# Experts 0 and 1: one x array with four tokens to a partition, loaded in two strided halves

## The chip, the cores and the metric

The kernel runs on one core of a Trainium2 chip. The metric is the device time of one execution in microseconds (us); lower is better. Every time below comes from runs on the chip or from one profiled execution of the kernel before.

## The reference

Eight experts, each a two-layer network with its own weights. Inputs are float32: x (8 x 256 x 512), w1 (8 x 512 x 2048), w2 (8 x 2048 x 512), b1 (8 x 2048), b2 (8 x 512).

```python
h = np.matmul(x, w1) + b1[:, np.newaxis, :]
h = np.maximum(h, 0)
return (np.matmul(h, w2) + b2[:, np.newaxis, :]).astype(np.float32)
```

The weights are 67 MB, 4.2 MB to each matrix; an x of one expert is 0.5 MB.

## The kernel before

**Weights.** GpSimd's queue loads every w1 and w2 by one DMA (the last two w2 by two), and the DMA casts float32 to float16 on the way. Three buffers each for w1 and w2 rotate (NW = 3), so a load of expert e >= 3 waits on GpSimd until TensorE is through with expert e - 3 (`load_w1`, `load_w2`, lines 147 to 162). The issue order of this queue is written out by hand in lines 164 to 175: w1 of 0, b2, w1 of 1, x of 2 and 3, w1 of 2, w1 of 3, w2 of 0, x of 4 to 7, w1 of 4, w2 of 1 and so on. The first of them waits for `s_first`, which ScalarE raises after its warm-up activation (line 126).

**x.** The x of experts 2 and 3 (one DMA) and of 4 to 7 (one DMA) also goes through GpSimd's queue, cast on the way. The x of experts 0 and 1 does not: SyncE loads it as float32 at the very start, one DMA of 512 KB for each expert (lines 129 to 131), two tokens to a partition, so that partition p of `x32[e]` holds tokens 2p and 2p + 1 in 4 KB. VectorE casts expert 0 (line 132) and ScalarE expert 1 (line 134).

**Turning x.** TensorE needs x with the hidden dimension on the partitions. `transposes(e)` (lines 108 to 123) does this on VectorE with 32 x 32 block transposes. `x16[e]` gives the array, its first partition and R, the tokens to a partition; one instruction turns R blocks by 4, so an expert takes T // R // 32 * 4 instructions: 16 for R = 2 (experts 0 and 1), 8 for R = 4 (experts 2 and 3), 4 for R = 8. Tokens come out in an order that depends on R, and `h_columns` (line 205) puts them in the order of the output when ScalarE evicts h.

**Order.** `transposes(0)` stands ahead of a section that is synchronised by hand (line 137), which every engine but GpSimd enters when the casts and turns ahead of it are done. In the section VectorE turns b1 (line 180), then x of expert 1, and in step s the x of expert s + 1 (line 201). Steps run from 0 to 10: step s does the first product of expert s (line 294, s < 8) and the second product of expert s - 3 (line 311, s >= 3); line 321 adds b2. SyncE stands between the DMAs and TensorE: in step s it waits for b2 (step 0), for the turned x (`s_xT`) and for w1 to land (line 235 in `go`), and then raises `s_go` for TensorE, which takes it in line 279. ScalarE evicts the first product with bias and ReLU (line 223) from four PSUM banks; its first eviction also waits for the turned b1. VectorE and ScalarE evict the second product (line 195). The results of experts 6 and 7 go into `x32[0]` and `x32[1]`, which are free by then (line 79), and are stored by SyncE (line 246); the results of 0 to 3 and of 4 and 5 are stored by two DMAs when the last weights are in (line 240).

Of the kernel before, what the change touches and what calls it, by code (L numbers as in the profile page):

```python
# [10 lines left out]
def kernel(  # L11
# [12 lines left out]
    nc = tc.nc  # L24
    fp32 = mybir.dt.float32
    fp16 = mybir.dt.float16
    relu = mybir.ActivationFunctionType.Relu
    PE = mybir.EngineType.PE
    E, T, H = x.shape
    M = w1.shape[2]  # L30
    P = 128
    nTB = T // P
# [15 lines left out]
    def sbuf(name, shape, dtype):  # L48
        return ctx.enter_context(nc.sbuf_tensor(name, shape, dtype))
# [11 lines left out]
    w2_sb = sbuf("w2_sb", [P, NW * nJ * H], fp16)  # L61
    xT = sbuf("xT", [P, 2 * nKC * T], fp16)
    hT = sbuf("hT", [P, (LAG + 1) * nJ * T], fp16)
    x32 = [sbuf(f"x32_{e}", [P, nTB, H], fp32) for e in range(2)]
    x16 = {}
    for e in range(2):
        x16[e] = (sbuf(f"x_{e}", [P, nTB, H], fp16), 0, nTB)
    x_group = {}
    for first, n in X_LOADS.items():
        R = n * T // P  # L70
# [3 lines left out]
    results = {}  # L74
    for first, n in GROUPS.items():
        t = sbuf(f"out_{first}", [P, n * nTB, H], fp32)
        for i in range(n):
            results[first + i] = t
    results[E - 2], results[E - 1] = x32
    ph = ctx.enter_context(nc.psum_tensor("ph", [P, NPH, H], fp32))  # L80
    po = ctx.enter_context(nc.psum_tensor("po", [P, 2 * nTB * H], fp32))

# [25 lines left out]
    def transposes(e):  # L108
        t, p0, R = x16[e]
        if e >= 2:  # L110
            first = max(f for f in X_LOADS if f <= e)
            nc.vector.wait_ge(landed[f"x{first}"], 16)
            nc.vector.wait_ge(s_ph, nJ * (e - 1))
        mine = xT[:, e % 2 * nKC * T : (e % 2 + 1) * nKC * T].rearrange("p (kc t) -> p kc t", kc=nKC)
        last = None
        for g in range(T // R // B):
            src = t[p0 + B * g : p0 + B * (g + 1)]
            for b in range(nB):
                last = nc.vector.transpose(  # L119
                    out=mine[b * B : (b + 1) * B].rearrange("p kc (r g i) -> p g r kc i", r=R, i=B)[:, g],  # L120
                    in_=src[:, :, b * (H // nB) : (b + 1) * (H // nB)].rearrange(
                        "p r (i kc) -> p r kc i", kc=nKC))
        return last
# [2 lines left out]
    tc.keep_in_program_order(nc.scalar.activation(out=warm[:], in_=ones1[:], func=relu).then_inc(s_first, 1))  # L126
    tc.keep_in_program_order(nc.scalar.dma_start(
        out=b1_rows[:], in_=b1.rearrange("e (b i) -> (e b) i", b=nB)))
    for e in range(2):
        tc.keep_in_program_order(nc.sync.dma_start(  # L130
            out=x32[e][:], in_=x[e].rearrange("(p tb) h -> p tb h", tb=nTB)))
    nc.vector.tensor_copy(out=x16[0][0][:], in_=x32[0][:])  # L132
    transposes(0)
    tc.keep_in_program_order(nc.scalar.copy(out=x16[1][0][:], in_=x32[1][:]))  # L134

    section = ctx.enter_context(ExitStack())
    by_hand = section.enter_context(tc.tile_critical(
# [17 lines left out]
    def load_w2(e):  # L155
# [5 lines left out]
        for lo, hi in zip(cuts, cuts[1:]):  # L161
# [5 lines left out]
         in_=b2.rearrange("e h -> (e h)").rearrange("(o f) -> o f", o=1))  # L167
# [11 lines left out]
    for b in range(nB):  # L179
        turned = nc.vector.transpose(  # L180
            out=b1T[b * B : (b + 1) * B, nB - 1 - b : nB - 1 - b + nJ * B],
            in_=b1_rows[:].rearrange("r (i j) -> r j i", j=nJ),
# [31 lines left out]
    for s in range(E + LAG):  # L214
        if s < E:
            if s > LAG:
                nc.scalar.wait_ge(s_po, nTB * (s - LAG))
            for j in range(nJ):
# [5 lines left out]
                    out=dst,  # L224
                    in_=src,
# [22 lines left out]
    for s in range(E + LAG):  # L248
# [5 lines left out]
        e = s - LAG  # L254
# [114 lines left out]
```

## Time and profile before

| | |
|---|---|
| time, median of 3 runs | 180.75 us (180.69 to 181.15) |
| the profiled execution, its own time | 180.72 us |
| its span in the trace | 178.9 us |
| TensorE busy | 135.3 us, 76% |
| VectorE busy | 65.1 us, 36% |
| ScalarE busy | 75.4 us, 42% |
| DMA moved | 40.46 MB, mean 226 GB/s |

The span runs from the first to the last instruction that the profile holds; 1.8 us of the run lie outside it. In the profile, PE is TensorE's matmul, PEld its weight load, DVE is VectorE, ACT ScalarE, POOL GpSimd and SP SyncE; a "q" behind a name is that engine's sequencer. A group shows its line, engine, operation, output <- input and count; then its busy time, the mean duration in ns of one, and the idle time of the engine ahead of it with what ended that. GB/s counts the bytes as written, so a casting load reads twice what it shows.

### The profile page before, as it was taken

Reading aid. Unit: us, or ns where it says so; the run is one execution under the profiler, and the core shown is the slowest. Engines: PE = TensorE matmul, PEld = TensorE weight load, DVE = VectorE, ACT = ScalarE, POOL = GpSimd, SP = SyncE. Lnnn points to the kernel's source line nnn. Section 1 sums busy time; section 2 is a strip of 40 time slices with the busy share of each in tenths; the row PEclk is TensorE's granted clock in tenths of the full one; section 3 lists DMA queues with packets and bytes.
Section 4 is the critical chain, followed back from the end, with each engine's and each line's share of the span. In section 5 each row is a group of like instructions: output and inputs, shape, how many; then the busy total and the mean of one; then the engine's idle time right before and its main releaser. Section 6 shows DMA issues by size and latency. Waiting matters only on the chain. (4 is left out here: it accounts for less than half of the span.)

```text
span 178.9 us, 2979 instructions
## 1 busy us (share of the span) xinstructions
PE 135.3 (76%) x784; PEld 93.5 (52%) x784; DVE 65.1 (36%) x92; ACT 75.4 (42%) x153; POOL 11.7 (7%) x25
## 2 busy tenths in 40 slices
PE   0003988868699890998978896889698896999990
PEld 0003878858698330794468643874298442434330
DVE  0989938475000299700088006910230003030100
ACT  3201596757777113483087505780387201020110
POOL 4200012020200101001010001000200002000000
PEclk9999999999999997599999999999999999799999
DMA  5989989999999998998999999999899899999996
GB/s 201 282 179 233 234 178 233 234 194 218 236 209 200 236 220 190 234 231 179 234 231 194 220 234 212 198 234 220 190 234 231 183 231 205 212 227 201 348 416 266
DMA packets 3826, 40.46 MB, mean 226 GB/s; under 512 B 448, under 2 KB 464, under 8 KB 1264
## 3 DMA queue, kind: packets, MB, share of 16 engines
q0 software_dynamic: 2912, 35.14, 92.5%
q1 hardware_dynamic: 864, 5.24, 7.2%
q10 hardware_dynamic: 48, 0.07, 0.1%
q14 instruction: 2, 0.02, 0.0%
HBM read 71.39 MB, written 4.19 MB: 422 GB/s over the span
## 5 line engine op out<-in xcount | busy, mean ns | idle before, releaser
L294 PE MATMUL ph<-xT,w_sb 128*128 x512 | 72.4, 303 | 33.1 <-PEq L279 30.2
L294 PEld LDWEIGHTS ph<-xT,w_sb 128*128 x512 | 66.8, 146 | 39.8 <-issue 29.1
L223 ACT ACTIVATE hT<-ph,b1T 128x256 f16<-128x256 f32 x128 | 60.1, 474 | 33.4 <-PE ph L294 29.8
L311 PE MATMUL po<-w_sb,hT 128*128 x256 | 58.3, 387 | 1.8 <-issue 1.8
L119 DVE STREAM_TRANSPOSE xT<-x 32x256 f16<-32x256 f16 (+2 forms) x64 | 45.0, 703 | 27.0 <-DMA x<-in_x_dram 22.4
L311 PEld LDWEIGHTS po<-w_sb,hT 128*128 x256 | 25.3, 99 | 34.1 <-issue 8.4
L195 DVE COPY out<-po 32x512 f32<-32x512 f32 (+1 forms) x20 | 13.7, 687 | 64.8 <-PE po L311 64.6
L195 ACT COPY out<-po 32x512 f32<-32x512 f32 (+1 forms) x20 | 11.5, 577 | 47.7 <-PE po L311 47.5
L88 POOL DMA_DIRECT2D w_sb<-in_w_dram x18 | 9.7, 541 | 137.2 <-PE po L311 71.4
L321 PE MATMUL po<-b_sb,ones 1*128 x16 | 4.8, 378 | 3.9 <-issue 2.5
L195 ACT COPY x<-po 128x512 f32<-128x512 f32 x2 | 1.2, 585 | 13.6 <-PE po L311 13.6
L195 DVE COPY x<-po 128x512 f32<-128x512 f32 x2 | 1.4, 692 | 13.3 <-PE po L311 13.3
L321 PEld LDWEIGHTS po<-b_sb,ones 1*128 1x128 f16 x16 | 1.3, 91 | 6.4 <-issue 6.1
L180 DVE STREAM_TRANSPOSE b1T<-b_rows 32x512 f32<-32x512 f32 x4 | 4.1, 1026 | 0.5 <-issue 0.5
L134 ACT CAST x<-x 128x1024 f16<-128x1024 f32 x1 | 1.0, 1044 | 3.4 <-DMA x<-in_x_dram 3.4
L132 DVE CAST x<-x 128x1024 f16<-128x1024 f32 x1 | 0.7, 695 | 3.2 <-DMA x<-in_x_dram 3.2
L126 ACT ACT_TABLE_LOAD x1 | 1.3, 1283 | 0.7 <-PEq L353 0.7
L88 POOL DMA_DIRECT2D x<-in_x_dram x2 | 1.3, 664 | 0.0
L88 POOL DMA_DIRECT2D b_sb<-in_b_dram x1 | 0.5, 499 | 0.0
L125 DVE MEMSET ones<- 1x128 f16 x1 | 0.2, 165 | 0.9 <-PEq L353 0.9
L126 ACT ACTIVATE warm<-ones 1x128 f16<-1x128 f16 x1 | 0.3, 309 | 0.0
L353 POOL MEMSET const-float32-0.0<- 128x1 f32 x1 | 0.1, 99 | 0.2 <-issue 0.2
(3 smaller groups left out, 0.3 us busy)
## 6 DMA issues: line engine op xcount, KB each, us to landing
w_sb<-in_w_dram POOLq DMA_DIRECT2D x14, 2048.0 KB, 41.1
w_sb<-in_w_dram POOLq DMA_DIRECT2D x2, 1024.0 KB, 27.1
out_dram<-out SPq DMA_DIRECT2D x1, 2048.0 KB, 7.2
w_sb<-in_w_dram POOLq DMA_DIRECT2D x1, 1536.0 KB, 17.7
x<-in_x_dram SPq DMA_DIRECT2D x2, 512.0 KB, 4.1
x<-in_x_dram POOLq DMA_DIRECT2D x1, 1024.0 KB, 34.3
out_dram<-out SPq DMA_DIRECT2D x1, 1024.0 KB, 9.3
out_dram<-x SPq DMA_DIRECT2D x2, 512.0 KB, 6.4
```

The source lines that it names most:

```text
L88: engine.dma_start(**kw).then_inc(landed[key], 16)
L119: last = nc.vector.transpose(out=mine[b * B : (b + 1) * B].rearrange("p kc (r g i) -> p g r kc i", r=R, i=B)[:, g], in_=src[:, :, b * (H / ...
L125: nc.vector.memset(ones1[:], 1.0)
L126: tc.keep_in_program_order(nc.scalar.activation(out=warm[:], in_=ones1[:], func=relu).then_inc(s_first, 1))
L132: nc.vector.tensor_copy(out=x16[0][0][:], in_=x32[0][:])
L134: tc.keep_in_program_order(nc.scalar.copy(out=x16[1][0][:], in_=x32[1][:]))
L180: turned = nc.vector.transpose(out=b1T[b * B : (b + 1) * B, nB - 1 - b : nB - 1 - b + nJ * B], in_=b1_rows[:].rearrange("r (i j) -> r j i" ...
L195: last = copy(out=results[e][at : at + rows, tb * n + k, :], in_=po[k * rows : (k + 1) * rows, bank : bank + H])
L223: nc.scalar.activation(out=dst, in_=src, func=relu, bias=b1T[:, bias_at : bias_at + 1], scale=1.0,).then_inc(s_credit, 1)
L294: last = nc.tensor.matmul(ph[:, j % NPH, 0:T], w1_sb[:, bass.ds(w_from + (kc * M + j), P, nJ)], xT[:, bass.ds(x_at + kc * T, T)], start=(k ...
L311: return nc.tensor.matmul(banks[tb], hT[:, bass.ds(h_from + (j * nTB + tb) * P, P)], w2_sb[:, bass.ds(w2_from + j * H, H)], start=False, s ...
L321: nc.tensor.matmul(banks[tb], ones1[:], b2_sb[:, bass.ds(s * H, H)], start=True, stop=False)
```

## The change

Both x arrays become one: `x32` and `x_0` have 128 partitions of four tokens. Partitions 0 to 63 hold expert 0 and partitions 64 to 127 expert 1; partition p holds tokens 4p to 4p + 3 of its expert. SyncE still issues two DMAs of 512 KB. The first takes rows 0 and 1 of each partition, the second rows 2 and 3, so each reads 128 runs of 4 KB that lie 8 KB apart, and each brings half of both experts. VectorE casts the first half and ScalarE the second, and `transposes(0)`, which now reads partitions 0 to 63 in all four rows, stands behind both casts. R becomes 4 for experts 0 and 1, so `transposes` issues 8 instructions of the 32 x 512 form for each instead of 16 of the 32 x 256 form. The results of experts 6 and 7 go into the two halves of `x32`.

```diff
-    x32 = [sbuf(f"x32_{e}", [P, nTB, H], fp32) for e in range(2)]
-    x16 = {}
-    for e in range(2):
-        x16[e] = (sbuf(f"x_{e}", [P, nTB, H], fp16), 0, nTB)
+    R0 = 2 * nTB
+    x32 = sbuf("x32", [P, R0, H], fp32)
+    x16_0 = sbuf("x_0", [P, R0, H], fp16)
+    x16 = {e: (x16_0, e * (P // 2), R0) for e in range(2)}
+    x_halves = [(r, r + nTB) for r in range(0, R0, nTB)]
...
-    results[E - 2], results[E - 1] = x32
+    for e, (lo, hi) in zip((E - 2, E - 1), x_halves):
+        results[e] = x32[:, lo:hi, :]
...
-    for e in range(2):
-        tc.keep_in_program_order(nc.sync.dma_start(
-            out=x32[e][:], in_=x[e].rearrange("(p tb) h -> p tb h", tb=nTB)))
-    nc.vector.tensor_copy(out=x16[0][0][:], in_=x32[0][:])
+    x_rows = x[0:2].rearrange("e (p r) h -> (e p) r h", r=R0)
+    for lo, hi in x_halves:
+        tc.keep_in_program_order(nc.sync.dma_start(out=x32[:, lo:hi, :], in_=x_rows[:, lo:hi, :]))
+    (lo, mid), (_, hi) = x_halves
+    nc.vector.tensor_copy(out=x16_0[:, lo:mid, :], in_=x32[:, lo:mid, :])
+    tc.keep_in_program_order(nc.scalar.copy(out=x16_0[:, mid:hi, :], in_=x32[:, mid:hi, :]))
     transposes(0)
-    tc.keep_in_program_order(nc.scalar.copy(out=x16[1][0][:], in_=x32[1][:]))
```

## The prediction

> **What bounds the kernel now.** I read the page's DMA part first, then the chain that ended last, and then the timeline of the places that the chain names.
>
> ```profile
> DMA  5989989999999998998999999999899899999996
> ...
> q0 software_dynamic: 2912, 35.14, 92.5%
> ...
> w_sb<-in_w_dram POOLq DMA_DIRECT2D x14, 2048.0 KB, 41.1
> ```
>
> The first row shows 40 slices of the span with the 16 DMA engines at nine tenths or nearly so in all but the first and the last. GpSimd's queue (q0) holds 92.5% of all engine time. A load of 2 MB lands 41.1 us (median) after its issue. The stretch from 59 to 110 us gives what one costs by itself (start and end, length, busy time of each engine, granted clock, DMA share, GB/s):
>
> ```profile
> 59.00:110.00 51.00, 41.57 (x230) 26.76 (x230) 21.24 (x22) 20.94 (x43) 2.41 (x5) 0.93 1.02 218
> ```
>
> The last number is 218 GB/s written, so 2.097 MB take 9.62 us, and a load that lands after 41 us had three others ahead of it. The queue does not run dry; the DMA engines set the pace. The chain agrees:
>
> ```profile
> 109.31 39.43 DMA w_sb<-in_w_dram
> ...
> 149.13 0.60 PE po L321 x2
> ...
> 149.99 8.77 PE po L311 x32
> ...
> 167.05 7.09 PE po L311 x32
> ...
> 174.17 0.69 DVE x L195
> ```
>
> The weight load issued at 109.31 lands at 148.74 (109.31 + 39.43), and three second products follow with hardly a gap. Earlier steps of TensorE wait for loads as well; the columns are start, duration, instruction and the idle time ahead of it:
>
> ```profile
> 71.89 9.74 PE L294 MATMUL ph<-xT,w_sb 128*128 x64 [4.97 <-PEq L279]
> ...
> 91.28 4.41 PE L294 MATMUL ph<-xT,w_sb 128*128 x32 [1.20 <-PEq L279]
> ...
> 110.64 4.41 PE L294 MATMUL ph<-xT,w_sb 128*128 x32 [1.62 <-PEq L279]
> ```
>
> Line 279 takes SyncE's go. The last two starts are 19.36 us apart, and two loads at 9.62 make 19.24. In front of step 4 TensorE sits idle for 4.97 us, against 1.20 in front of step 5: about 3.8 us of delay from the first four steps can vanish there. Near the end the same stream shows once more:
>
> ```profile
> 165.92 0.82 SPq L240 DMA_DIRECT2D out_dram<-out  x2
> ...
> 166.23 0.60 PE L321 MATMUL po<-b_sb,ones 1*128 x2
> ```
>
> The flush of line 240 stands behind the landing of w2 of expert 7, first part (its other wait, the eviction of expert 5, was over by 160.2, that is 158.79 + 1.39). So that landing is at 165.9, and TensorE wanted it at 166.23. **The time is the start of the DMA stream, plus its engine time, plus a tail of some 13 us.** A change on VectorE or ScalarE in the first 17 us counts only if it makes this stream start later or take longer.
>
> **The change part by part.** The stretch where it acts:
>
> ```profile
> 0.74 0.86 SPq L130 DMA_DIRECT2D x<-in_x_dram  x2
> ...
> 2.65 0.66 POOL L88 DMA_DIRECT2D w_sb<-in_w_dram  x1 [2.20 <-ACT warm L126]
> ...
> 4.31 0.69 DVE L132 CAST x<-x 128x1024 f16<-128x1024 f32 x1 [3.23 <-DMA x<-in_x_dram]
> 5.04 7.18 DVE L119 STREAM_TRANSPOSE xT<-x 32x256 f16<-32x256 f16 x16
> ...
> 5.78 1.04 ACT L134 CAST x<-x 128x1024 f16<-128x1024 f32 x1 [3.45 <-DMA x<-in_x_dram]
> 12.71 4.14 DVE L180 STREAM_TRANSPOSE b1T<-b_rows 32x512 f32<-32x512 f32 x4 [0.49 <-issue]
> ...
> 16.14 9.82 PE L294 MATMUL ph<-xT,w_sb 128*128 x64 [16.14 <-PEq L279]
> 16.89 7.20 DVE L119 STREAM_TRANSPOSE xT<-x 32x256 f16<-32x256 f16 x16
> 17.28 0.47 ACT L223 ACTIVATE hT<-ph,b1T 128x256 f16<-128x256 f32 x1 [10.45 <-PE ph L294]
> ...
> 27.51 4.38 PE L294 MATMUL ph<-xT,w_sb 128*128 x32 [1.55 <-PEq L279]
> ```
>
> *Casts.* They keep their shapes (128 x 1024), engines and prices, 0.69 and 1.04 us. What is new is that the first turn waits for both. ScalarE's ends at 5.78 + 1.04 = 6.82, so the turn starts near 6.9 instead of 5.04: +1.85 us.
>
> *Turns.* Sixteen of 32 x 256 become eight of 32 x 512, a form that experts 2 and 3 have already:
>
> ```profile
> L119 DVE STREAM_TRANSPOSE xT<-x 32x256 f16<-32x256 f16 x32 | 14.0, 436 | 0.5
> L119 DVE STREAM_TRANSPOSE xT<-x 32x512 f16<-32x512 f16 x16 | 11.3, 703 | 7.3 <-PE ph L294 3.7 <-DMA x<-in_x_dram 3.4
> ```
>
> Eight at 703 ns are 5.62 us against 7.18: -1.56. The turned x of expert 0 is ready at 6.9 + 5.62 = 12.5 instead of 12.22, 0.3 us later. Behind it on VectorE stands b1's turn, which ends at 17.15 instead of 16.85 and on which ScalarE's first eviction waits; that one starts at 17.28 for TensorE's sake, so it hardly moves. Then expert 1 is turned by 17.2 + 5.62 = 22.8 instead of 24.09, and TensorE asks for it at 27.51. What hides the 0.3 us is SyncE's wait for weights, as its waits in the first 20 us show:
>
> ```profile
> SPq L364 <- DVE xT L119: 6.4, 1, 6.4
> ...
> SPq L235 <- DMA w_sb<-in_w_dram: 2.9, 1, 2.9
> ```
>
> SyncE enters the section when the first turn is done (6.4 us of waiting) and then waits 2.9 us more for w1 of expert 0. So the first matmul does not move for the first 2.9 us of a late turn. If that cover were gone, the next is the 3.8 us in front of step 4. VectorE's net 2.8 us saved also buys nothing: what follows there waits for x of 2 and 3 (3.4 us of the idle above).
>
> *ScalarE's evictions* read PSUM in another column order for experts 0 and 1, that of experts 2 and 3. All 128 of them cost the same, whatever their expert, so this is nothing:
>
> ```profile
> L223 ACT ACTIVATE hT<-ph,b1T x128: 473/473/476, 17.3 to 139.3; 128x256 f16<-128x256 f32 x128
> ```
>
> *The stores* of experts 6 and 7 read 4 KB from each partition, as before: nothing. GpSimd's issue order and its first wait (ScalarE's warm-up) stay.
>
> *The two loads.* This is the only edit that touches the stream. Bytes and run length stay (4 KB), the gap between runs is new: 8 KB from run to run, and no row of before shows a load with holes. What the two loads take of the engines, by the queue part for 0 to 6 us, and what stores of the same queue take, by that for 150 to 179 us:
>
> ```profile
> q1 hardware_dynamic: 288, 1.05, 49.3%
> ```
> ```profile
> q1 hardware_dynamic: 576, 4.19, 34.4%
> ```
>
> 49.3% of 6 us are 2.96 us of all 16 engines for 1.05 MB; 34.4% of 29 us are 9.98 for 4.19 MB, or 2.50 for 1.05. From below, then, the loads could reach the rate of the stores and give back 0.46 us. From above, I let a hole as long as a run cost as much as reading it: the engine time doubles, +2.96 us. Both go straight onto the stream. I take 0, by the nearest rows: the weight loads, whose partitions start 32 KB apart, hold 218 GB/s written (436 read), and each 4 KB run was a packet of its own already (288 for 256 runs).
>
> The Trainium skill has a rule against this ("DMA: Bandwidth & Descriptors", section "Latency and other measured facts"): row pitches that are large powers of two slow a copy, there to 103 instead of 214 GB/s per direction at a pitch of 4 MiB. By that ratio, an estimate, the loads would take 2.1 times as long, +3.2 us. Its pitches begin at 512 KiB, and this trace's 32 KB pitch shows no such loss.
>
> **Sum.** 180.72 us (the profiled run) = 178.9 of span + 1.82 around it. Wait for both casts +1.85, turns -1.56, both under the 2.9 us of cover: 0. Loads: 0. That gives 180.72, which agrees with the median of 180.75; I forecast **180.8**, as the runs shown reach further up than down.
>
> **The rivals.**
>
> *The strided loads are slower (slower).* The place is the stretch from 2 to 6 us, the price up to +2.96 us, or 183.7; half of that holes' cost gives +1.5, or 182.2. It decides once the loads take over 3.5 us of all engines instead of 2.96. For it: nothing waits between these bytes and the weights behind them. Against it: the rows above, and that 1.05 MB are 1.5% of what the stream reads.
>
> *The late turn becomes the bound.* It would have to slip by more than 2.9 us to move the first matmul and by 2.9 + 3.8 = 6.7 to move the end. Even with the loads doubled, the second half lands some 3 us later, so the turn ends at 15.5 and step 0 moves by under 1 us: nothing more than the loads' own price.
>
> *The clock dips elsewhere (slower).* The 32 matmuls at 149.99 took 8.77 us against 7.09 at 167.05; the clock granted was 0.54 there:
>
> ```profile
> 152.00:155.00 3.00, 3.00 (x9) 1.13 (x8) 0.00 (x0) 0.00 (x0) 0.00 (x0) 0.54 1.04 216
> ```
>
> Today a landing at 165.9 hides nearly all of that; without the dip 0.3 us would be won (166.23 to 165.92). If it fell behind 167, the end would come 1.7 - 0.3 = 1.4 us later: 182.1. Nothing in the change moves it that I can see.
>
> *The stream gets shorter (faster).* The loads reach the stores' rate (-0.46) and the dip misses the tail (-0.3): 180.0. The first alone gives 180.3, inside what a measurement of this kernel can tell from no change, which is about 0.3%, or 0.54 us.
>
> *The edit does not do what it says.* The built program has two load DMAs of 128 x 1024 and eight turns for each expert, so this is out.
>
> **How the numbers follow.** No change: 0.62. Strided loads slower by over 0.54 us: 0.20. Dip in the last product: 0.05. Faster by over 0.54: 0.13, for the two gains together and for what the profile does not show of the first 6 us. So faster 0.13, same 0.62, slower 0.25. The range runs from 180.1, just above the faster case, to 182.0, into the nearer half of the two slower ones; about 0.05 lie below and 0.13 above.
>
> **What would show it.** Right: the first turn starts near 6.9 and eight of them take 5.6 us; the first matmul stays near 16.1, step 4 near 71.9, the last weight wait ends near 148.7; q1 takes about half of the engines up to 6 us. Wrong: ScalarE's cast starting well after 5.8 (slow loads), and all later landings shifted by one amount; or landings unmoved and the tail behind 149 longer (clock); or a first matmul released by VectorE.

## The result and the profile after

The changed kernel takes 181.53 us (median, 181.35 to 182.11) against 180.71 for the kernel before, measured beside it: a ratio of 1.0049, 95% interval 1.0037 to 1.0061. It is slower by 0.8 us. The profiled execution, the fastest of its six runs, took 181.35 us with a span of 179.6, that is 0.63 us over the 180.72 of before.

The start of the changed kernel's timeline, in the rows that answer to those shown of before:

```profile
0.74 0.86 SPq L133 DMA_DIRECT2D x<-in_x_dram  x2
...
2.65 0.66 POOL L90 DMA_DIRECT2D w_sb<-in_w_dram  x1 [2.20 <-ACT warm L128]
...
4.95 0.69 DVE L135 CAST x<-x 128x1024 f16<-128x1024 f32 x1 [3.87 <-DMA x<-in_x_dram]
6.45 1.04 ACT L136 CAST x<-x 128x1024 f16<-128x1024 f32 x1 [4.12 <-DMA x<-in_x_dram]
7.53 5.71 DVE L121 STREAM_TRANSPOSE xT<-x 32x512 f16<-32x512 f16 x8 [1.88 <-ACT x L136]
13.73 4.15 DVE L183 STREAM_TRANSPOSE b1T<-b_rows 32x512 f32<-32x512 f32 x4 [0.49 <-issue]
...
16.84 9.72 PE L297 MATMUL ph<-xT,w_sb 128*128 x64 [16.84 <-PEq L282]
17.92 5.72 DVE L121 STREAM_TRANSPOSE xT<-x 32x512 f16<-32x512 f16 x8
17.98 0.47 ACT L226 ACTIVATE hT<-ph,b1T 128x256 f16<-128x256 f32 x1 [10.48 <-DVE b1T L183]
```

The x loads and the first weight load are issued where they were, to 0.01 us. But both casts, which wait for the two halves of x, come late by nearly the same amount: 4.95 against 4.31 and 6.45 against 5.78. From the first matmul on, everything is shifted: 16.84 against 16.14. The later gates (start, duration, idle ahead of it) say that the shift stays:

```profile
72.44 9.95 PE L297 MATMUL ph<-xT,w_sb 128*128 x64 [4.90 <-PEq L282]
...
91.92 4.41 PE L297 MATMUL ph<-xT,w_sb 128*128 x32 [1.22 <-PEq L282]
...
111.27 4.40 PE L297 MATMUL ph<-xT,w_sb 128*128 x32 [1.62 <-PEq L282]
...
150.63 7.08 PE L314 MATMUL po<-w_sb,hT 128*128 x32 [0.26 <-issue]
...
166.56 0.82 SPq L243 DMA_DIRECT2D out_dram<-out  x2
166.79 0.60 PE L324 MATMUL po<-b_sb,ones 1*128 x2 [1.14 <-SPq L239]
```

Step 4 starts 0.55 us later than before, steps 5 and 6 by 0.64 and 0.63, and the flush behind the last weights (166.56 against 165.92) by 0.64. The idle times ahead of the gates have hardly moved (4.90 against 4.97, 1.22 against 1.20, 1.62 against 1.62): TensorE waits as it did, for the same stream, which runs 0.64 us late. The dip of the clock is absent from these three last products (7.08 against 8.77 in the first of them), and that wins nothing: TensorE then waits 1.14 us for the last go.

Where the stream lost it shows in the stretch from 2 to 4 us. First the row of before, then that of the changed kernel; the last two numbers are the DMA share and GB/s:

```profile
2.00:4.00 2.00, 0.00 (x0) 0.00 (x0) 0.00 (x0) 0.33 (x2) 1.35 (x3) 1.00 0.87 346
```
```profile
2.00:4.00 2.00, 0.00 (x0) 0.00 (x0) 0.00 (x0) 0.33 (x2) 1.35 (x3) 1.00 0.92 252
```

The engines were not idler (0.92 against 0.87), yet they moved 252 GB/s instead of 346. SyncE's queue in the same 2 us, again before and then after (packets, MB, share of 16 engines):

```profile
q1 hardware_dynamic: 169, 0.63, 78.2%
```
```profile
q1 hardware_dynamic: 124, 0.48, 88.2%
```

Before, 0.63 MB took 78.2% of 2 us, or 2.5 us of all engines for one MB; after, 0.48 MB took 88.2%, or 3.7. The packets themselves take longer: 148 ns each before (78.2% of 2 us on 16 engines, shared by 169), 228 ns after. By 4 to 5 us that is nearly over: 0.33 MB at 96.1%, or 2.9 us for one MB, against 0.36 MB at 97.5%, or 2.7. The weights come later for it: from 4 to 5 us GpSimd's queue starts its first two packets before, and none after.

### The profile page after: what moved, and what is told of

It reads as the page before. It is cut to its first block, busy times and chain, and to the rows that moved or that the text cites. A ratio compares the mean times of both kernels' runs of the same rounds, so it can differ in the third digit from the quotient of the medians.

```text
span 179.6 us, 2964 instructions
## 1 busy us (share of the span) xinstructions
PE 133.9 (75%) x784; PEld 93.0 (52%) x784; DVE 62.4 (35%) x76; ACT 75.6 (42%) x153; POOL 11.8 (7%) x25
## 5 line engine op out<-in xcount | busy, mean ns | idle before, releaser
L314 PE MATMUL po<-w_sb,hT 128*128 x256 | 56.6, 379 | 2.2 <-issue 2.2
L121 DVE STREAM_TRANSPOSE xT<-x 32x512 f16<-32x512 f16 (+1 forms) x48 | 42.3, 881 | 29.6 <-DMA x<-in_x_dram 23.5
```

Of the source, the lines that this page charges most:

```text
L121: last = nc.vector.transpose(out=mine[b * B : (b + 1) * B].rearrange("p kc (r g i) -> p g r kc i", r=R, i=B)[:, g], in_=src[:, :, b * (H / ...
L314: return nc.tensor.matmul(banks[tb], hT[:, bass.ds(h_from + (j * nTB + tb) * P, P)], w2_sb[:, bass.ds(w2_from + j * H, H)], start=False, s ...
```

## The experiments

The theory: holes in the first reads slow the opening of the DMA stream, and the whole kernel slides by that. The rivals: the program's own changes (turn behind both casts) cost the time; a pitch that is a power of two; a lower rate of the engines for all reads with holes. Ratios are to the kernel before, beside it on the same chip, with the 95% interval.

### Holes alone, and the rest of the change alone

```diff
     for e in range(2):
         tc.keep_in_program_order(nc.sync.dma_start(
-            out=x32[e][:], in_=x[e].rearrange("(p tb) h -> p tb h", tb=nTB)))
+            out=x32[e][:], in_=x_rows[:, nTB * e : nTB * (e + 1), :]))
```

Here `x_rows` is x of experts 0 and 1 with four tokens to a row, as in the changed kernel.

> The kernel before with only its two first loads changed: each reads 128 runs of 4 KB that lie 8 KB apart, as the changed kernel does. Casts, turns and all else are those of before, so x of experts 0 and 1 holds the tokens of both, mixed. If the holes in the reads cost the time: 181.3 to 181.6 us, both halves land 0.6 us later than in the profile of before (casts near 4.95 and 6.45), the first matmul 0.7 us later. If the cost lies in the changed program (its order of casts and turns, or how its code is fetched): 180.7, casts at 4.3 and 5.8.

Measured: 181.75 us, ratio 1.0054 (1.0035 to 1.0073), a little over the first forecast, with the casts at 5.28 and 6.71 and the first matmul at 17.21.

The counterpart, made from the changed kernel:

```diff
-    for lo, hi in x_halves:
-        tc.keep_in_program_order(nc.sync.dma_start(out=x32[:, lo:hi, :], in_=x_rows[:, lo:hi, :]))
+    for e, (lo, hi) in enumerate(x_halves):
+        tc.keep_in_program_order(nc.sync.dma_start(
+            out=x32[:, lo:hi, :], in_=x[e].rearrange("(p tb) h -> p tb h", tb=nTB)))
```

> The changed kernel with its loads put back to contiguous reads: load e takes the 512 KB of expert e, two tokens to a partition, into rows 2e and 2e + 1. Casts and turns are those of the changed kernel, so the tokens of experts 0 and 1 are mixed. If the holes cost the time: 180.7 us, casts near 4.3 and 5.8, first turn near 6.9. If the rest of the changed program does: 181.5.

Measured: 180.71 us, ratio 0.9993 (0.9985 to 1.0002). Its timeline:

```profile
4.03 0.69 DVE L136 CAST x<-x 128x1024 f16<-128x1024 f32 x1 [2.95 <-DMA x<-in_x_dram]
...
5.53 1.04 ACT L137 CAST x<-x 128x1024 f16<-128x1024 f32 x1 [3.19 <-DMA x<-in_x_dram]
6.61 5.71 DVE L121 STREAM_TRANSPOSE xT<-x 32x512 f16<-32x512 f16 x8 [1.88 <-ACT x L137]
12.81 4.14 DVE L184 STREAM_TRANSPOSE b1T<-b_rows 32x512 f32<-32x512 f32 x4 [0.49 <-issue]
16.07 4.14 PE L298 MATMUL ph<-xT,w_sb 128*128 x20 [16.07 <-PEq L283]
```

The first turn waits 1.88 us for ScalarE's cast, as in the changed kernel, and the first matmul is at 16.07. So the holes carry all of the loss that can be measured, and the casts, the turns and the eight instructions saved for each expert carry none, neither way. Its casts start 0.28 and 0.25 us ahead of those of the kernel before, with the same contiguous loads: by so much two profiles can differ.

### Other pitches

The edit is that of the first run, with 6 and with 16 tokens to a row of `x_rows` instead of 4, over experts 0 to 2 and 0 to 7.

> As the kernel before, but each load reads 128 runs of 4 KB that lie 12 KB apart (tokens of experts 0 to 2, mixed). If a pitch that is a power of two is what hurts: 180.7 us. If any hole hurts: as with 8 KB or a little more, 181.3 to 182.0. If the change costs by something else than its reads: 180.7.

Measured: 181.80 us, ratio 1.0050 (1.0031 to 1.0069).

> As the kernel before, but each load reads 128 runs of 4 KB that lie 32 KB apart (tokens of all experts, mixed). If the cost is a conflict that grows with a pitch that is a power of two: clearly over the run with 8 KB, 182 us or more. If the hole costs the same whatever its length: 181.3 to 181.6, as with 8 KB. If the reads cost nothing: 180.7.

Measured: 181.43 us, ratio 1.0030 (1.0020 to 1.0040). A pitch of 12 KB costs what 8 KB costs, and 32 KB no more than that. The power of two falls as a cause, and so does a loss that grows with the hole. The rule of the Trainium skill that the prediction weighed ("DMA: Bandwidth & Descriptors", "Latency and other measured facts") begins at 512 KiB; no run here bears out an extension of it down to 8 KB.

### The first load or the second

```diff
     for e in range(2):
+        src = x_rows[:, nTB * e : nTB * (e + 1), :] if e == 0 else x[e].rearrange("(p tb) h -> p tb h", tb=nTB)
         tc.keep_in_program_order(nc.sync.dma_start(
-            out=x32[e][:], in_=x[e].rearrange("(p tb) h -> p tb h", tb=nTB)))
+            out=x32[e][:], in_=src))
```

> The kernel before with holes in its first load alone: it reads 128 runs of 4 KB that lie 8 KB apart, the second load stays contiguous (tokens of expert 0 are wrong). If holes lower the rate of the engines evenly: half of the loss, 181.1 to 181.2 us, and the second cast no later than the first is. If the loss is paid only where the stream starts, in the first two or so us after the first packet: the whole of it, 181.4 to 181.7, both casts late by the same 0.6 to 1.0 us.

Measured: 181.79 us, ratio 1.0060 (1.0048 to 1.0072).

The mirror has `e == 1` in that line.

> The mirror of the run before: the first load contiguous, the second with holes of 4 KB (tokens of expert 1 are wrong). If holes lower the rate evenly: 181.1 to 181.2 us, first cast at 4.3 and second 0.4 later than 5.8. If only the start of the stream pays: 180.7, casts at 4.3 and 5.8.

Measured: 180.93 us, ratio 1.0012 (1.0002 to 1.0023). The stretches from 2 to 4 us, the first load with holes and then the second:

```profile
2.00:4.00 2.00, 0.00 (x0) 0.00 (x0) 0.00 (x0) 0.33 (x2) 1.35 (x3) 1.00 0.87 219
```
```profile
2.00:4.00 2.00, 0.00 (x0) 0.00 (x0) 0.00 (x0) 0.33 (x2) 1.35 (x3) 1.00 1.00 369
```

The first load alone brings the whole loss, 219 GB/s in the opening and both casts late (5.09 and 6.87), although the second load is contiguous; the same holes in the load that is issued 0.4 us later cost 0.1%. That rules out an even loss of rate, where each load would have cost about half.

The second load might have been cheap because rows beside its own had just been read. In the next run it takes rows of experts 6 and 7:

```diff
+    x_rows = x[6:8].rearrange("e t h -> (e t) h").rearrange("(p r) h -> p r h", r=4)
     for e in range(2):
+        src = x_rows[:, 0:nTB, :] if e == 1 else x[e].rearrange("(p tb) h -> p tb h", tb=nTB)
...
```

> As the run with holes in the second load alone, but that load reads rows of experts 6 and 7, which nothing has read before (tokens of expert 1 are wrong). If only the opening of the stream pays for holes: 180.8 to 181.0 us, as there, second cast near 5.85. If the second load was cheap because its neighbourhood in memory had been read already: 181.2 to 181.7, second cast 0.4 us or more late.

Measured: 180.89 us, ratio 1.0010 (1.0001 to 1.0019), second cast at 5.75. What was read before plays no part that can be seen: it is the opening that pays.

### Without holes: one load, or a load for each expert

```diff
-    for lo, hi in x_halves:
-        tc.keep_in_program_order(nc.sync.dma_start(out=x32[:, lo:hi, :], in_=x_rows[:, lo:hi, :]))
+    tc.keep_in_program_order(nc.sync.dma_start(out=x32[:], in_=x_rows))
```

> The changed kernel with its two loads made one: 128 partitions of 8 KB, contiguous, 1 MB. Both casts wait for all of it. If only holes cost: 180.7 us, the first cast some 1.5 us later than before and the time not moved by that. If a late cast or turn counts at all: over 181.

Measured: 181.00 us, ratio 1.0015 (1.0005 to 1.0026). VectorE's cast starts at 5.86, 1.55 us later than before, and the kernel is 0.2 us slower, between the two cases that were expected. It keeps the layout of the change and avoids most of its loss; faster than before it is not. What the 0.2 us are is not shown; holes, of which this load has none, they are not.

```diff
-    for lo, hi in x_halves:
-        tc.keep_in_program_order(nc.sync.dma_start(out=x32[:, lo:hi, :], in_=x_rows[:, lo:hi, :]))
+    for p in (0, P // 2):
+        tc.keep_in_program_order(nc.sync.dma_start(out=x32[p : p + P // 2], in_=x_rows[p : p + P // 2]))
...
+    nc.vector.tensor_copy(out=x16_0[: P // 2], in_=x32[: P // 2])
+    tc.keep_in_program_order(nc.scalar.copy(out=x16_0[P // 2 :], in_=x32[P // 2 :]))
```

> The changed kernel with its loads and casts cut by expert instead of by row: 64 partitions of 8 KB each, contiguous, and each cast takes 64 partitions of 2048 elements. The first turn waits for VectorE's own cast only. If only holes cost: 180.7 us, the same as the kernel before although x is turned earlier and VectorE does 8 fewer instructions for each of the two experts. If turning x early is worth anything: under 180.2. If 64 partitions load slower than 128: over 181, casts late.

Measured: 182.92 us, ratio 1.0112 (1.0097 to 1.0127).

```profile
5.89 1.22 DVE L134 CAST x<-x 64x2048 f16<-64x2048 f32 x1 [4.81 <-DMA x<-in_x_dram]
7.14 5.71 DVE L121 STREAM_TRANSPOSE xT<-x 32x512 f16<-32x512 f16 x8
8.23 1.89 ACT L135 CAST x<-x 64x2048 f16<-64x2048 f32 x1 [5.89 <-DMA x<-in_x_dram]
```

Reads without holes, and yet the worst run, as was expected in case that 64 partitions load slower than 128. 512 KB into 64 partitions land by 5.89 where 128 partitions have them by 4.31, the second half by 8.23 instead of 5.78. The Trainium skill advises against transfers to partition halves and for one of 128 partitions ("DMA: Bandwidth & Descriptors", "Rules for kernel authors"); this run agrees, at 2.1 us here. Whether the 64 partitions or the 8 KB runs in them do it was not taken apart, but the single load above has runs of 8 KB too and loses far less.

### More reads in flight at the opening

The second load goes to ScalarE's queue ahead of its warm-up; in the kernel before:

```diff
+    tc.keep_in_program_order(nc.scalar.dma_start(
+        out=x32[1][:], in_=x[1].rearrange("(p tb) h -> p tb h", tb=nTB)))
     tc.keep_in_program_order(nc.scalar.activation(out=warm[:], in_=ones1[:], func=relu).then_inc(s_first, 1))
...
-    for e in range(2):
+    for e in range(1):
```

> The kernel before with its second first load issued by ScalarE ahead of its warm-up instead of by SyncE: both contiguous loads are in flight about 0.45 us sooner. If the opening of the stream is short of reads in flight: 180.2 to 180.6 us and more than 270 GB/s from 2 to 3 us. If each engine's own first reads are slow however many are queued: 180.7. The warm-up comes 0.4 us later, and with it the first weight load; if that counts, 181.0 to 181.2.

Measured: 181.26 us, ratio 1.0030 (1.0019 to 1.0042); 276 GB/s from 2 to 4 us against 346. Two queues at once did not open the stream faster, and the first weight load is issued at 3.08 instead of 2.65; how much of the 0.6 us (181.26 less 180.67) is due to which was not separated.

The same move in the changed kernel:

> The changed kernel with its second load issued by ScalarE ahead of its warm-up, both with holes. If the loss comes from too few reads in flight at the opening: it shrinks, 180.9 to 181.2 us. If reads with holes are slow there however many are queued: 181.4 to 181.6, or 0.3 more by the later first weight load.

Measured: 181.33 us, ratio 1.0029 (1.0017 to 1.0042), between the first two cases that were expected. Next to its contiguous twin the holes cost nothing that can be measured, and 295 GB/s are no less than the twin's 276. Both opened slowly, though, so this doesn't show that more reads in flight cure anything.

```diff
-    nc.gpsimd.wait_ge(s_first, 1)
     load_w1(0)
```

> The changed kernel without GpSimd's wait for ScalarE's warm-up, so that the first weight load is issued near 0.5 us instead of 2.65 and its contiguous reads share the engines with the x loads from the start. If the loss is engine time that the loads with holes leave unused while nothing else is queued: the weights fill it, 180.7 us or less, first w1 landing before 16.1. If the x loads are then so late that the first turn becomes the bound: first matmul released by the turn, 181 or more. If the loss stays with the loads whatever runs beside them: 181.5.

Measured: 181.66 us, ratio 1.0051 (1.0037 to 1.0065): no better than the changed kernel. The first weight load is issued at 1.23 instead of 2.65, but the x loads take the engines as before (2 to 4 us):

```profile
q1 hardware_dynamic: 114, 0.45, 88.6%
```

The x packets take 88.6% of the engines, and the weight load does not fill the rest: although it is issued 1.4 us sooner, none of its packets starts before 5.5 us, when the x loads are nearly through. In the changed kernel the first five start between 5.0 and 5.5. So the weights' start follows the x loads and not their own issue, and giving them more time ahead wins nothing.

### All profiles in one row of numbers

The flush of line 240 (243 after) starts when the last gating weights have landed. In each profiled execution:

| kernel | first cast | first matmul | flush | its own time | time less flush |
|---|---|---|---|---|---|
| before | 4.31 | 16.14 | 165.92 | 180.72 | 14.80 |
| after | 4.95 | 16.84 | 166.56 | 181.35 | 14.79 |
| kernel before, pitch 8 KB | 5.28 | 17.21 | 166.84 | 181.65 | 14.81 |
| kernel before, pitch 12 KB | 4.99 | 17.82 | 167.43 | 182.24 | 14.81 |
| kernel before, pitch 32 KB | 4.64 | 17.23 | 167.13 | 181.94 | 14.81 |
| holes in the first load | 5.09 | 17.33 | 166.99 | 181.79 | 14.80 |
| holes in the second load | 4.41 | 16.40 | 166.10 | 180.89 | 14.79 |
| second load from other rows | 4.33 | 16.25 | 166.27 | 181.09 | 14.82 |
| changed kernel, contiguous | 4.03 | 16.07 | 165.95 | 180.74 | 14.79 |
| one load | 5.86 | 16.80 | 166.44 | 181.22 | 14.78 |
| a load for each expert | 5.89 | 18.19 | 168.18 | 182.97 | 14.79 |
| kernel before, two queues | 5.84 | 16.62 | 166.40 | 181.22 | 14.82 |
| changed kernel, two queues | 5.57 | 17.09 | 166.84 | 181.63 | 14.79 |
| changed kernel, first weights sooner | 5.05 | 17.21 | 166.83 | 181.65 | 14.82 |

The time is the landing of the last weights plus 14.8 us, within 0.02, whatever was done to the first 8 us. The delay is complete with the first weights: the flush is late by what the first matmul is late, to 0.25 us. The first cast, in contrast, does not rank the kernels (the single load, the pitch of 32 KB). Where SyncE issues two loads of 128 partitions, it starts at 4.03 to 4.41 if the first of them is contiguous, and at 4.64 to 5.28 if that one has holes.

## Why the prediction was right or wrong

**What bounds the kernel: right.** The start of the stream, its engine time and a fixed tail make the time; the last column above shows the tail. The tail from the flush is 14.8 us of run time: the 13 us of the span and the 1.8 around it.

**Casts and turns: right.** Eight turns took 5.71 us (5.62 forecast), and the first began 0.04 after ScalarE's cast. With contiguous reads it began at 6.61 and b1's turn at 12.81 (0.1 us later than before). The turn's cover was to shrink by 0.3 us from 2.9, and SyncE's wait for w1 of expert 0 did so in the changed kernel, where the end of the turn and the landing had both slipped (by 1.0 and 0.7 us):

```profile
SPq L367 <- DVE xT L121: 6.8, 1, 6.8
...
SPq L238 <- DMA w_sb<-in_w_dram: 2.6, 1, 2.6
```

The run with contiguous reads, 0.9993, shows that the sum of these edits is nothing, and that VectorE's savings are worth nothing here.

**Evictions and stores: right.** The 128 evictions cost 475 ns in the mean (474 before), and from flush to end no time was gained or lost.

**The two loads: wrong.** "I take 0, by the nearest rows: the weight loads" is the step that failed. The weight loads have no holes, and their 218 GB/s are those of a stream that has long been running. The loads of x run in the opening, and there the prediction's own rows already said that other terms hold: 2.96 us of all engines for 1.05 MB are 2.8 us for one MB, where the stream reads one MB in 2.1 (0.93 of the engines at 436 GB/s). Every landing behind the opening inherits what is lost in it. The row of 49.3% (2.96 us) became:

```profile
q1 hardware_dynamic: 288, 1.05, 56.7%
```

That is 3.40 us of all engines, +0.44, inside the bounds of -0.46 and +2.96 that were kept for the range; the landings slipped by 0.64. The sign that the prediction named for this case came as described: ScalarE's cast starts well after 5.8 (6.45), and the later landings are shifted by one amount. The point from which this rival was to decide, 3.5 us of engine time, was set a little too high: it counts what the packets take up to 6 us and not when the weights behind them land.

**The forecast.** The likeliest case, no change (0.62), did not come; the rival of slower strided loads (0.20) did, at about half of its middle price (0.6 to 0.8 us of 1.5). 181.53 lies inside 180.1 to 182.0, because the range kept part of the way to the bound of the unknown price; where in it the time would fall, the prediction could not say. The late turn stayed under its cover. The dip of the clock did miss the last products, but the 0.3 us allowed for that were not won: the last second product starts 1.13 us behind the flush with the dip (167.05 less 165.92) and without it (167.69 less 166.56).

**What stays open.** That the first load pays and the second hardly does is shown. Whether it pays for coming first in its queue or for running in the first microseconds was not separated. Why the first packets with holes take half as long again is not shown either; neither the pitch, nor its being a power of two, nor fresh memory, nor the issue time of the weights explains it. In the runs with pitches of 12 and 32 KB the first matmul came later still (17.82 and 17.23) than the casts (4.99 and 4.64) account for. The profile shows a part of it: the weight packets that start by 6 us took 1.41 us each with 12 KB (14 packets in 20.5% of 6 us on 16 engines) and 1.31 with 32 KB, against 1.24 before. Both of these profiled executions were also slower than the median of their kernel (182.24 to 181.80, 181.94 to 181.43).

## What to carry to other kernels

Where a DMA stream sets the pace from end to end, the bytes that open it are on the critical path even when nothing waits for them: read them in contiguous runs, with all 128 partitions, and do the reordering later or elsewhere. Price a load by rows from the same part of the run, since the rate of a full stream says little about its first microseconds. Work saved on an engine that waits for that stream was worth nothing here, and one kernel with the loads of the one version and the arithmetic of the other shows it at once.

## What the runs showed of the hardware

- Holes of 4 to 28 KB between first reads of 4 KB cost 0.3 to 0.6% of 180.7 us, that is 0.5 to 1.1 us; holes of 4 KB in the load issued 0.4 us later, alone, cost 0.1%.
- A load of 512 KB into 64 partitions (runs of 8 KB), first in the queue, landed 1.6 us later than one into 128 (runs of 4 KB), and a pair of them cost 2.1 us.
- SyncE's and ScalarE's queues issuing at once opened the stream no faster than SyncE's alone, in one trace of each: 276 GB/s from 2 to 4 us against 346.
- GpSimd's first weight load, issued at 1.23 us instead of 2.65 while the x loads were under way, started no packet before 5.5 us.
